# A lasting tile for the gates' weights, and decode states updated by GpSimd in whole quarters, in a hybrid mLSTM, retention and HGRN2 step

## The chip, the cores and the metric

The kernel runs on one core of one Trainium2 chip. Its engines are named as in the profile: PE multiplies matrices (PEld is its loading of weights), DVE is VectorE, ACT ScalarE, POOL GpSimd, and SP holds the queue that issues all loads and stores. The metric is the device time of one execution in microseconds (us), lower is better. Lines are those of the kernel before, unless it is said that they are of the new one, whose lines are some eight higher behind the middle of the file.

## The reference

One step of a trunk of two layers, for a prompt of 1024 tokens and for 8 sequences that decode one token each, with the same weights. Each layer projects its input once, runs three groups of heads side by side, gates them, projects the result and adds it with a LayerNorm. Shortened to what bears on the change:

```python
proj = jnp.einsum('btd,dn->btn', x, w_in)
(m_qk, m_v, m_o, m_z, m_if, r_q, r_k, r_v, r_g,
 h_f, h_i, h_q, h_g) = jnp.split(proj, _split_points(), axis=-1)
...
gates = (m_if + b_mgate).astype(f32)          # 4 heads, i and f
ig = gates[..., :M_HEADS]
lf_m = jax.nn.log_sigmoid(gates[..., M_HEADS:])
...
# mLSTM, one step (for a decoded token L = 1)
dec = jnp.exp(b[..., -1] + m - m_new)
w_s = jnp.exp(b[..., -1:] - b + igT - m_new[..., None])
C_new = dec[..., None, None] * C + jnp.einsum('bhs,bshk,bshv->bhkv', w_s, k, v)
...
# HGRN2, one step
S_new = (jnp.exp(Bc[:, -1])[..., None] * S
         + jnp.einsum('bshk,bshv->bhkv', k * jnp.exp(Bc[:, -1:] - Bc), v))
...
mix = jnp.concatenate([y_m, y_r, y_h], axis=-1).astype(x.dtype)
out = jnp.einsum('btm,md->btd', mix, w_out)
x_new = layer_norm(ALPHA * x + out, ln_g, ln_b)
```

For a decoded token the output of a head is its new state, read with the query: a sum over the key index for every value index.

## The kernel before

The prompt is worked off in two blocks, b = 0 (512 tokens and the 8 decoded ones, 520 columns in two runs of 260) and b = 1 (512 tokens). A list of sixteen steps sets their order: the three groups H (HGRN2), R (retention) and M (mLSTM) of a layer and block, and the output projections, each put between groups of the next block. In the M step of block 0 all mLSTM prompt work and its decode are issued; the chunks of 128 tokens of that step (four, `L632` scores, `L644`, `L643` and `L647` products, `L613`, `L619` transposes) then run on PE among the projections of the H step of block 1.

A tile framework gives every tile a buffer of its tag (`NBUF` says how many) and sets the waits; a scheduler that models time sets the order of each engine's instructions, and each engine then follows its own list. All loads and stores are issued in order on SP.

`project` multiplies the block's input, which is held as two rounded parts, with one 128-column tile of weights, held as two parts too: three matmul terms for each of 8 slices (`L150`). Its weights come as two halves through `load_w`: load to "st", copy on ACT (`L133`), difference on DVE (`L134`), into one of three "w" buffers, asked for ahead of the rest (`AHEAD_W`). `silu_to` takes a result out of its PSUM bank (ACT `L216`, DVE `L217`). The "gate path" below is the stretch of the M step's last projections before the chunks, with `L217` and `L588` on DVE.

`gates` is called once for each layer and block, four times. It takes one "w" buffer, clears it on POOL (`L240`), copies the 8 gate columns into it on ACT (`L242`) and their rounding error on DVE (`L243`), and multiplies (`L251`).

The decode states are worked off in quarters (a head, or a pair of half heads, by four of the eight sequences). For mLSTM, `sample_M` has 8 quarters a layer of 96 partitions x 384: it loads the state `St` and the rows of q and k, broadcast over the partitions from the DRAM tile `drow` that `token_rows` wrote (PE transposes `L694`, ACT copy, stores); POOL multiplies k by v (`L829`), DVE does `St*w + kv` for each of four sequences (`L831`), the state is stored, and DVE multiplies by q and sums in one instruction for each of four sequences (`sample_read`, `L714`, with a small read of the sum behind each). A quarter takes three of the four "smp" buffers. `sample_H` has 4 quarters a layer of 128 x 256: two products on POOL (`L744`, `L745`), the sum on DVE (`L746`), the same reading. `sample_R` is of the same shape and is not changed.

The sums of all quarters of a group are transposed, normed and gated by its `fin`, which is put into `late` and run in the H step of block 1, after its projections: PE transposes `L753`, `L778`, `L839`. Norms take the power -1/2 on POOL (`L162`). In a chunk of mLSTM POOL also does the two `L638`, and ACT `L607` and DVE `L627` read the "mb" tiles that are loaded from the DRAM tile `db`.

In HGRN2's recurrence for the prompt, DVE and PE take turns (`L391`, `L392` and `L376`), with `L463` and `L464` on POOL behind `L457` and `L458`; its tiles are of the tags "hc" and "hg". "c15" is a tag of 128 x 388 tiles for norms and token rows, "gt" one for gates' columns.

## Time and profile before

| | us |
|---|---|
| median of 3 runs | 1347.32 |
| lowest and highest | 1344.84, 1353.62 |
| the profiled execution | 1354.15 |
| its span, first to last instruction | 1352.4 |
| PE busy in it | 1286.7 |
| DVE busy | 876.2 |
| ACT busy | 593.7 |
| POOL busy | 256.2 |

The profile shows one execution, which took some 7 us more than the median. In it the mean clock granted to PE was 0.983 of the full one. In the timelines of the trace each row begins with the start and the duration in us, neighbours of one kind are put together with their count, and what stands in brackets is how long the engine was idle before and what ended it.

### The profile page before, as it was taken

The page shows a single profiled execution, that of the slowest core. Times are in us where ns is not written, and L with a number is a line of the kernel's source. Part 1 is how long each engine was busy: PE and PEld are TensorE (multiplying, and loading weights), DVE is VectorE, ACT ScalarE, POOL GpSimd, SP SyncE. Part 2 cuts the span into 40 slices and gives each one's busy share as a digit, 9 for nine tenths or more (in the row PEclk, how much of TensorE's full clock was granted, in tenths as well). Part 3 has the DMA queues.
Part 4 walks back from the last instruction along what each step waited for, and adds up shares of the span by engine and source line. Part 5 has one row for each costly group of instructions (what it writes and reads, how often), then busy time and mean ns, then how long its engine had stood idle before and what let it go on. Part 6 is the DMA issues. An engine that isn't in the chain of part 4 may idle for free. (4 is left out here: it accounts for less than half of the span.)

```text
span 1352.4 us, 30892 instructions
## 1 busy us (share of the span) xinstructions
PE 1286.7 (95%) x11888; PEld 1168.9 (86%) x11888; DVE 876.2 (65%) x2548; ACT 593.7 (44%) x1301; POOL 256.2 (19%) x261
## 2 busy tenths in 40 slices
PE   7979999988999999999999999999799999999986
PEld 7979999877898888889987999989688987888886
DVE  6566468568665656747745765875776549475775
ACT  6522455428432234736723234653564232454441
POOL 0012023012200330102210232210221014111223
PEclk9998999999999999999999999999998999999998
DMA  4543245543333452422254344555343335333252
GB/s 156 154 133 94 79 132 146 181 134 103 111 104 103 130 152 79 136 95 72 84 179 154 99 115 145 145 177 156 112 134 96 97 124 157 97 102 95 87 176 94
DMA packets 113835, 166.21 MB, mean 123 GB/s; under 512 B 21092, under 2 KB 49924, under 8 KB 113688
## 3 DMA queue, kind: packets, MB, share of 16 engines
q1 hardware_dynamic: 113688, 164.25, 39.7%
q8 instruction: 93, 1.52, 0.5%
q14 instruction: 54, 0.44, 0.1%
HBM read 140.90 MB, written 15.32 MB: 116 GB/s over the span
## 5 line engine op out<-in xcount | busy, mean ns | idle before, releaser
L150 PE MATMUL pp<-x,w 128*128 128x260 f32 (+2 forms) x6096 | 1022.9, 324 | 25.0 <-DVE w L134 5.6
L150 PEld LDWEIGHTS pp<-x,w 128*128 128x128 f32 x6096 | 874.5, 191 | 111.4 <-DVE w L134 9.1
L134 DVE TENSOR_TENSOR w<-st,w 128x512 fp32r<-128x512 f32 x344 | 251.7, 733 | 172.2 <-ACT w L133 166.9
L133 ACT CAST w<-st 128x512 fp32r<-128x512 f32 x344 | 212.6, 621 | 329.5 <-PE pp L150 279.1
L162 POOL TENSOR_TENSOR small<-small,phalf 128x4 f32<-128x4 f32 (+1 forms) x54 | 62.4, 1158 | 376.7 <-DVE small L193 193.6
L181 ACT ACTIVATE c<-pa,small,small 128x96 f32<-128x96 f32 (+1 forms) x144 | 49.9, 427 | 18.6 <-DVE small L178 18.6
L551 DVE SCALAR_TENSOR_TENSOR tmp<-tmp,prm,tmp 128x512 f32<-128x512 f32 x72 | 53.4, 742 | 3.1 <-ACT tmp L543 2.6
L831 DVE SCALAR_TENSOR_TENSOR smp<-smp,swb,smp 96x96 f32<-96x96 f32 x64 | 21.1, 378 | 39.3 <-POOL smp L829 39.3
L376 PEld LDWEIGHTS pa<-hc,hc 64*32 64x32 f32 (+1 forms) x2432 | 32.1, 109 | 16.6 <-issue 9.3
L376 PE MATMUL pa<-hc,hc 64*32 64x32 f32 (+1 forms) x2432 | 38.2, 199 | 7.3 <-DVE hc L392 5.2
L210 DVE SCALAR_TENSOR_TENSOR y<-pf,prm,y 128x128 f32<-128x128 f32 (+1 forms) x132 | 36.5, 327 | 12.8 <-PE pf L204 12.4
L216 ACT ACTIVATE tmp<-pp 128x260 f32<-128x260 f32 (+1 forms) x48 | 21.8, 455 | 42.0 <-PE pp L150 40.3
L880 DVE SCALAR_TENSOR_TENSOR y<-tmp,pp 128x260 f32<-128x260 f32 (+2 forms) x56 | 25.5, 456 | 19.9 <-PE pp L150 18.6
L463 POOL TENSOR_TENSOR x<-x 128x520 f32<-128x520 f32 (+1 forms) x12 | 16.1, 1344 | 115.3 <-DVE x L457 101.2
L829 POOL TENSOR_TENSOR smp<-smp,svs 96x384 f32<-96x384 f32 x16 | 13.2, 823 | 130.9 <-DMA smp<-drow 123.8
L941 ACT ACTIVATE t<-pa,small 128x512 f32<-128x512 f32 (+1 forms) x27 | 19.9, 774 | 40.8 <-DVE small L931 40.8
L217 DVE SCALAR_TENSOR_TENSOR y<-tmp,pp 128x260 f32<-128x260 f32 (+1 forms) x48 | 24.1, 503 | 20.2 <-ACT tmp L216 20.2
L379 DVE COPY_PREDICATED dscores<-lmask,pa 128x128 f32<-128x128 uint8 x96 | 26.9, 296 | 15.1 <-PE pa L376 14.7
L157 POOL TENSOR_TENSOR x<-y,x 128x512 fp32r<-128x512 f32 (+1 forms) x20 | 24.1, 1219 | 65.4 <-ACT x L156 65.4
L714 DVE SCALAR_TENSOR_TENSOR smp<-smp,smp 96x96 f32<-96x96 f32 (+1 forms) x160 | 33.7, 253 | 0.2
L457 DVE TENSOR_TENSOR x<-pp,tmp 128x260 f32<-128x260 f32 (+1 forms) x36 | 17.9, 510 | 24.0 <-DMA x<-x 15.8
L204 PE MATMUL pf<-ident,c 128*128 128x128 f32 (+1 forms) x132 | 29.6, 272 | 3.0 <-DVE c L196 3.0
(245 smaller groups left out, 1649.4 us busy)
## 6 DMA issues: line engine op xcount, KB each, us to landing
st<-in_w_in_dram SPq DMA_DIRECT2D x280, 256.0 KB
st<-in_w_out_dram SPq DMA_DIRECT2D x72, 256.0 KB
smp<-drow SPq DMA_DIRECT2D x64, 144.0 KB
tmp<-xres SPq DMA_DIRECT2D x16, 260.0 KB
mb<-db SPq DMA_DIRECT2D x16, 256.0 KB
tmp<-in_xT_dram SPq DMA_DIRECT2D x16, 256.0 KB
xres<-rc SPq DMA_DIRECT2D x16, 256.0 KB
out_y_prompt_dram<-t SPq DMA_DIRECT2D x16, 256.0 KB
```

The source lines that it names most:

```text
L133: A.copy(out=w[:, 0], in_=st)
L134: V.tensor_sub(out=w[:, 1], in0=st, in1=w[:, 0].bitcast(F32))
L150: PE.matmul(p, lhsT=w[k // 4][:, wp, k % 4, :], rhs=xt[:, xp, k, c0:c1], start=(k == order[0] and i == 0), stop=(k == order[-1] and i == 2))
L162: G.tensor_tensor(out=r[:n, 0:4], in0=val, in1=phalf[:n], op=ALU.pow)
L181: A.activation(out=y[:n, 96 * h:96 * h + 96], in_=ht[:, h, :], func=AF.Identity, scale=rs[:n, h:h + 1], bias=ve[:n, 4 + h:5 + h])
L204: PE.transpose(py[:, 128 * j:128 * j + n], y[:n, 128 * j:128 * j + 128], ident[:n, :n])
L210: V.scalar_tensor_tensor(out=dst, in0=py[:, 128 * j:128 * j + n], scalar=prm[:, l, pc + j:pc + j + 1], in1=dst, op0=ALU.mult, op1=ALU.mult)
L376: PE.matmul(pz[z:z + w, i, :], lhsT=k_[r, j, o + z:o + z + w], rhs=q_[r, j, o + z + d:o + z + d + w], start=True, stop=True)
L379: V.copy_predicated(Dg, lmask[:, (LEVELS + (0,)).index(h), :].unsqueeze(1).to_broadcast([128, 4, 32]), pz)
L551: V.scalar_tensor_tensor(out=acc[:, 0:512], in0=raw[:, q:q + 512], scalar=cw(q), in1=acc[:, 0:512], op0=ALU.mult, op1=ALU.add)
L714: V.scalar_tensor_tensor(out=qb[:, i, :], in0=qb[:, i, :], scalar=1.0, in1=St[:, i, :], op0=ALU.mult, op1=ALU.mult, accum_out=hs[:, i:i + 1])
L880: V.scalar_tensor_tensor(out=r2[k][:, c0:c1], in0=xr[:, c0 - r0:c1 - r0], scalar=ALPHA, in1=p, op0=ALU.mult, op1=ALU.add)
```

## The change

There are three parts. The gates' weights get a tile of their own, 128 x 8 x 100, which is cleared once at the program's start; the columns of the 8 gates are filled for block 0 of each layer and stay for block 1. In `sample_H` and `sample_M` the state is updated on POOL with operations on whole quarters, and read with one product on POOL and one sum on DVE (`sample_read_pool`, new line 718 and 719); the decay of mLSTM is a product with a broadcast column (`rows_by`, new line 723). And four tags get another number of buffers: mb 2 to 3, c15 6 to 4, hc 4 to 3, gt 2 to 1.

```diff
-NBUF = dict(pp=3, pa=4, pf=1, t2=7, tmp=4, rc=3, mb=2, c15=6, smp=4, small=10, mv=4, bst=4, hc=4, hg=2, vv=1, st=3, w=3,
-            eb=2, gt=2, mpb=2, stg=1)
+NBUF = dict(pp=3, pa=4, pf=1, t2=7, tmp=4, rc=3, mb=3, c15=4, smp=4, small=10, mv=4, bst=4, hc=3, hg=2, vv=1, st=3, w=3,
+            eb=2, gt=1, mpb=2, stg=1)
...
     def gates(l, b, xt):
         n = width(b)
-        with tc.high_priority(offset=AHEAD_W):
-            stg = mk([128, KT, 8], "stg", NBUF["stg"])
-            dma(out=stg, in_=I["w_gate"][l])
-            w = mk([128, KT, 128], "w", NBUF["w"], dt=F32R)
-            G.memset(w.bitcast(F32), 0.0)
-            for i in range(2):
-                A.copy(out=w[:, :, 32 * i:32 * i + 4], in_=stg[:, :, 4 * i:4 * i + 4])
-                V.tensor_sub(out=w[:, :, 64 + 32 * i:68 + 32 * i], in0=stg[:, :, 4 * i:4 * i + 4],
-                             in1=w[:, :, 32 * i:32 * i + 4].bitcast(F32))
+        w = wgate
+        if b == 0:
+            with tc.high_priority(offset=AHEAD_W):
+                stg = mk([128, KT, 8], "stg", NBUF["stg"])
+                dma(out=stg, in_=I["w_gate"][l])
+                for i in range(2):
+                    A.copy(out=w[:, :, 32 * i:32 * i + 4], in_=stg[:, :, 4 * i:4 * i + 4])
+                    V.tensor_sub(out=w[:, :, 64 + 32 * i:68 + 32 * i], in0=stg[:, :, 4 * i:4 * i + 4],
+                                 in1=w[:, :, 32 * i:32 * i + 4].bitcast(F32))
...
+    def sample_read_pool(hs, r, St, qb, n):
+        G.tensor_mul(out=qb, in0=qb, in1=St)
+        V.tensor_reduce(out=hs, in_=qb, axis=AX.X, op=ALU.add)
+
+    def rows_by(t, v, r, n):
+
+        G.tensor_tensor(out=t, in0=t, in1=v.unsqueeze(2).to_broadcast([r, 4, n]), op=ALU.mult)
...
                 G.tensor_mul(out=St, in0=St, in1=eb)
-                V.tensor_add(out=St, in0=St, in1=kb)
+                G.tensor_add(out=St, in0=St, in1=kb)
                 dma(out=O["hgrn_s"][l, j, hf], in_=St)
-                sample_read(hs[:, j, bs], 128, St, qb, DK)
+                sample_read_pool(hs[:, j, bs], 128, St, qb, DK)
...
-                for i in range(4):
-                    V.scalar_tensor_tensor(out=St[:, i, :], in0=St[:, i, :], scalar=wb[0:96, h, 0, 4 * hf + i:4 * hf + i + 1],
-                                           in1=kb[:, i, :], op0=ALU.mult, op1=ALU.add)
+                rows_by(St, wb[0:96, h, 0, bs], 96, DH)
+                G.tensor_add(out=St, in0=St, in1=kb)
                 dma(out=O["mC_s"][l, h, hf], in_=St)
-                sample_read(hs[0:96, h, bs], 96, St, qb, DH)
+                sample_read_pool(hs[0:96, h, bs], 96, St, qb, DH)
...
+    wgate = cp.tile([128, KT, 100], F32R, name="wgate")
+    G.memset(wgate.bitcast(F32), 0.0)
```

Since a scheduler sets the orders, the change also moves what it doesn't name. On POOL in layer 0 the decode quarters stood among the gate path and the first two chunks, with the gates' memset behind the sixth. Before, from the fifth quarter (new buffers have new numbers; `x` is the output projection's input, `rc` belongs to a chunk):

```order
L829 TENSOR_TENSOR smp_4333<-smp_4333,svs_3932 96x384
L157 TENSOR_TENSOR x_776_5574<-y_16_194,x_776_5574 128x512
L157 TENSOR_TENSOR x_776_5574<-y_195_1598,x_776_5574 128x512
L829 TENSOR_TENSOR smp_4349<-smp_4349,svs_3932 96x384
L240 MEMSET w_4475 128x1024
L162 TENSOR_TENSOR small_4001<-small_3999,phalf 128x4
L638 TENSOR_TENSOR rc_4018<-t_368_2785,rc_4018 96x256
L638 TENSOR_TENSOR rc_4018<-t_369_2786,rc_4018 96x256
L829 TENSOR_TENSOR smp_4365<-smp_4365,svs_3932 96x384
L829 TENSOR_TENSOR smp_4381<-smp_4381,svs_3932 96x384
L162 TENSOR_TENSOR small_4084<-small_4082,phalf 128x4
```

In the new kernel the same place begins behind the input of the output projection, and reads (L837 is the old L829, L839 the sum into the state):

```order
L157 TENSOR_TENSOR x_773_5526<-y_194_1590,x_773_5526 128x512
L837 TENSOR_TENSOR smp_4261<-smp_4261,svs_3924 96x384
L723 TENSOR_TENSOR smp_4271<-smp_4271,swb_3886 96x384
L839 TENSOR_TENSOR smp_4259<-smp_4259,smp_4261 96x384
L718 TENSOR_TENSOR smp_4260<-smp_4260,smp_4259 96x384
L162 TENSOR_TENSOR small_3993<-small_3991,phalf 128x4
L638 TENSOR_TENSOR rc_4010<-t_367_2777,rc_4010 96x256
L638 TENSOR_TENSOR rc_4010<-t_368_2778,rc_4010 96x256
L837 TENSOR_TENSOR smp_4273<-smp_4273,svs_3924 96x384
L723 TENSOR_TENSOR smp_4283<-smp_4283,swb_3886 96x384
L839 TENSOR_TENSOR smp_4271<-smp_4271,smp_4273 96x384
L718 TENSOR_TENSOR smp_4272<-smp_4272,smp_4271 96x384
```

The memset is gone; a whole quarter, with the next one's product L723 drawn into it, stands before each chunk's power L162, and the eight quarters lie over the four chunks.

On DVE, the gate path of layer 0 (L217 and L588 empty the projections' banks, L134 makes weights) had the third and fourth quarter's updates and reads in it:

```order
L831 SCALAR_TENSOR_TENSOR smp_4299<-smp_4299,swb_3894,smp_4301 96x96 x4
L714 SCALAR_TENSOR_TENSOR smp_4300,shs_580_4266<-smp_4300,smp_4299 96x96 x4
L217 SCALAR_TENSOR_TENSOR y_375_2792<-tmp_3784,pp_3759 128x260
L134 TENSOR_TENSOR w_3822<-st_3820,w_3822 128x512
L217 SCALAR_TENSOR_TENSOR y_375_2792<-tmp_3812,pp_3787 128x260
L831 SCALAR_TENSOR_TENSOR smp_4315<-smp_4315,swb_3894,smp_4317 96x96 x3
L134 TENSOR_TENSOR w_4403<-st_4401,w_4403 128x512
L831 SCALAR_TENSOR_TENSOR smp_4315<-smp_4315,swb_3894,smp_4317 96x96
L714 SCALAR_TENSOR_TENSOR smp_4316,shs_580_4266<-smp_4316,smp_4315 96x96 x4
L588 SCALAR_TENSOR_TENSOR y_375_2792<-tmp_3850,y_375_2792 128x260
L134 TENSOR_TENSOR w_4408<-st_4406,w_4408 128x512
L588 SCALAR_TENSOR_TENSOR y_375_2792<-tmp_3878,y_375_2792 128x260
```

The same projections in the new order:

```order
L217 SCALAR_TENSOR_TENSOR y_374_2784<-tmp_3776,pp_3751 128x260
L134 TENSOR_TENSOR w_3814<-st_3812,w_3814 128x512
L217 SCALAR_TENSOR_TENSOR y_374_2784<-tmp_3804,pp_3779 128x260
L134 TENSOR_TENSOR w_4363<-st_4361,w_4363 128x512
L588 SCALAR_TENSOR_TENSOR y_374_2784<-tmp_3842,y_374_2784 128x260
L134 TENSOR_TENSOR w_4368<-st_4366,w_4368 128x512
L588 SCALAR_TENSOR_TENSOR y_374_2784<-tmp_3870,y_374_2784 128x260
L134 TENSOR_TENSOR w_4399<-st_4397,w_4399 128x512
L622 TENSOR_TENSOR c_520_3949<-pa_3945,gt_386 128x288
L624 TENSOR_SCALAR c_520_3949<-pa_3945,gt_386 128x96
L634 TENSOR_TENSOR mb_3931<-pa_3957,mb_3931 128x512
```

No decode instruction is left between them. The eight sums L719 stand later, one or two a chunk; the first of them is the third row here, among the statistics (L171) of the first chunk:

```order
L171 BN_AGGR mv_3982<-bst_3981 128x2 x3
L719 TENSOR_REDUCE shs_579_4258<-smp_4260 96x4
L627 SCALAR_TENSOR_TENSOR mb_4174<-mb_4174,gt_386,negm 128x128
L176 SCALAR_TENSOR_TENSOR small_3991<-small_3977,mv_3982 128x4
L627 SCALAR_TENSOR_TENSOR mb_4174<-mb_4174,gt_386,negm 128x128 x2
L609 COPY small_4015<-rc_4010 96x4
L627 SCALAR_TENSOR_TENSOR mb_4174<-mb_4174,gt_386,negm 128x128
L134 TENSOR_TENSOR w_4504<-st_4502,w_4504 128x512
L178 SCALAR_TENSOR_TENSOR small_3991<-mv_3982,small_3993 128x4
```

So behind the chunk's statistics a wait for POOL's first quarter now stands ahead of the mask L627 and of L176, the input of the norm's power.

On PE in layer 0, the transposes of the decode's q rows (pa_3901) and k rows (pa_3912) stood together, ahead of the gate path's last projections:

```order
L150 MATMUL pp_3523<-x_1_66,w_3492 128x260 x12
L694 MATMUL pa_3901<-ident,t_368_2785 8x96 x2
L694 MATMUL pa_3901<-ident,t_369_2786 8x96 x2
L694 MATMUL pa_3912<-ident,t_370_2787 8x96
L150 MATMUL pp_3561<-x_1_66,w_3553 128x260 x2
L694 MATMUL pa_3912<-ident,t_370_2787 8x96
L694 MATMUL pa_3912<-ident,t_371_2788 8x96 x2
L613 MATMUL pa_3948<-ident,vv_2789 128x128 x2
L150 MATMUL pp_3561<-x_1_66,w_3553 128x260 x10
```

Now those of the k rows (pa_3904) stand behind all of them, right before the first chunk's L632:

```order
L150 MATMUL pp_3845<-x_1_66,w_3814 128x260 x12
L694 MATMUL pa_3904<-ident,t_369_2779 8x96 x2
L694 MATMUL pa_3904<-ident,t_370_2780 8x96 x2
L613 MATMUL pa_3940<-ident,vv_2781 128x128 x3
L619 MATMUL pa_3945<-ident,t_369_2779 128x128 x2
L619 MATMUL pa_3945<-ident,t_370_2780 128x128
L632 MATMUL pa_3957<-t_367_2777,t_369_2779 128x128 x2
L632 MATMUL pa_3957<-t_368_2778,t_370_2780 128x128 x2
```

What moved is the start of the k rows: in the trace of before they stood 35 us ahead of the first L632 (252.6 against 287.88 us). At the second chunk the gates of block 1 stood so before:

```order
L150 MATMUL pp_4447<-x_428_3266,w_4444 128x512 x7
L632 MATMUL pa_4042<-t_368_2785,t_370_2787 128x128 x2
L632 MATMUL pa_4042<-t_369_2786,t_371_2788 128x128 x2
L150 MATMUL pp_4447<-x_428_3266,w_4444 128x512 x5
L251 MATMUL pp_4486<-x_428_3266,w_4475 100x512 x10
L643 MATMUL pa_4050<-Cst_167,rc_4018 128x97
L251 MATMUL pp_4486<-x_428_3266,w_4475 100x512 x2
```

and now so:

```order
L150 MATMUL pp_4407<-x_427_3258,w_4404 128x512 x12
L251 MATMUL pp_4438<-x_427_3258,wgate 100x512 x3
L632 MATMUL pa_4034<-t_367_2777,t_369_2779 128x128 x2
L632 MATMUL pa_4034<-t_368_2778,t_370_2780 128x128 x2
L251 MATMUL pp_4438<-x_427_3258,wgate 100x512 x8
L643 MATMUL pa_4042<-Cst_169,rc_4010 128x97
```

The gates read the lasting tile, and a part of them runs ahead of the chunk's scores. Ahead of the final transposes (L753 before, L761 in the new kernel) PE now has 14 more of the projections' 512-column matmuls. On SP the loads of the decode quarters and those of weights, about two a quarter, now take turns over the four chunks, and in the gate path only weights are loaded.

## Rows read from the trace of the kernel before

**Rows 1.** The page's busy time, share and instructions of each engine.

```profile
PE 1286.7 (95%) x11888; PEld 1168.9 (86%) x11888; DVE 876.2 (65%) x2548; ACT 593.7 (44%) x1301; POOL 256.2 (19%) x261
```

**Rows 2.** The list of PE's waits: for whom, us in total, times, longest.

```profile
PE pp L251 <- DVE small L178: 7.4, 2, 3.9
```

**Rows 3.** Timeline of PE, layer 0: start, us, what, idle before and its releaser.

```profile
252.20 0.41 PE L694 MATMUL pa<-ident,t 96*8 96x96 f32 x3
...
266.70 11.94 PE L150 MATMUL pp<-x,w 128*128 128x260 f32 x94 [0.41 <-DVE y L217]
281.95 6.10 PE L150 MATMUL pp<-x,w 128*128 128x260 f32 x36 [3.31 <-DVE y L217]
287.88 1.06 PE L632 MATMUL pa<-t,t 96*128 96x128 f32 x8
...
307.48 3.93 PE L251 MATMUL pp<-x,w 128*100 128x512 f32 x10 [3.50 <-DVE small L178]
...
340.20 4.66 PE L150 MATMUL pp<-x,w 128*128 128x512 f32 x19
...
358.60 0.38 PE L753 MATMUL pa<-ident,shs 128*8 128x128 f32 x2
```

**Rows 4.** Timeline of PE at the same place of layer 1.

```profile
936.47 4.55 PE L150 MATMUL pp<-x,w 128*128 128x260 f32 x36 [0.70 <-DVE y L217]
...
962.24 4.10 PE L251 MATMUL pp<-x,w 128*100 128x512 f32 x10 [3.89 <-DVE small L178]
```

**Rows 5.** Two stretches: us, busy PE, PEld, DVE, ACT, POOL, granted clock, DMA.

```profile
283.30:286.60 3.30, 3.30 (x17) 3.30 (x17) 0.54 (x3) 0.47 (x2) 0.82 (x1) 0.50 0.53 164
...
962.50:965.80 3.30, 3.30 (x9) 2.28 (x8) 1.46 (x4) 3.27 (x7) 2.22 (x3) 0.50 0.60 187
```

**Rows 6.** Timeline of POOL in layer 0.

```profile
263.29 0.82 POOL L829 TENSOR_TENSOR smp<-smp,svs 96x384 f32<-96x384 f32 x1 [26.14 <-DMA smp<-drow]
...
303.05 0.82 POOL L829 TENSOR_TENSOR smp<-smp,svs 96x384 f32<-96x384 f32 x1 [7.13 <-DMA smp<-in_s_C_dram]
303.81 0.95 POOL L240 MEMSET w<- 128x1024 f32 x1
...
317.69 0.82 POOL L829 TENSOR_TENSOR smp<-smp,svs 96x384 f32<-96x384 f32 x1 [7.04 <-DMA smp<-drow]
```

**Rows 7.** Timeline of ACT around the second block's gates, layer 0.

```profile
304.95 1.28 ACT L607 ACTIVATE rc<-mb,mpb 96x128 f32<-96x128 f32 x4 [3.35 <-DMA mb<-db]
306.14 0.32 ACT L242 CAST w<-stg 128x32 fp32r<-128x32 f32 x2
```

**Rows 8.** Timeline of DVE in the gate path of layer 0.

```profile
265.07 0.53 DVE L815 TENSOR_REDUCE sden<-c 8x4 f32<-8x384 f32 x1
...
279.84 1.00 DVE L831 SCALAR_TENSOR_TENSOR smp<-smp,swb,smp 96x96 f32<-96x96 f32 x4 [5.28 <-POOL smp L829]
...
281.48 0.42 DVE L217 SCALAR_TENSOR_TENSOR y<-tmp,pp 128x260 f32<-128x260 f32 x1
```

**Rows 9.** DVE's instructions by line and form: count, busy us, mean ns, idle.

```profile
L714 DVE SCALAR_TENSOR_TENSOR smp<-smp,smp 96x96 f32<-96x96 f32 x128 | 26.4, 246 | 0.1
...
L831 DVE SCALAR_TENSOR_TENSOR smp<-smp,swb,smp 96x96 f32<-96x96 f32 x64 | 21.1, 378 | 39.3 <-POOL smp L829 39.3
```

**Rows 10.** Timeline of all engines, HGRN2 recurrence of layer 0.

```profile
125.54 0.69 DVE L134 TENSOR_TENSOR w<-st,w 128x512 fp32r<-128x512 f32 x1 [1.89 <-ACT w L133]
...
127.57 1.31 POOL L463 TENSOR_TENSOR x<-x 128x520 f32<-128x520 f32 x1 [6.29 <-DVE x L457]
127.69 1.74 DVE L134 TENSOR_TENSOR w<-st,w 128x512 fp32r<-128x512 f32 x1
```

**Rows 11.** Timeline of all engines at an HGRN2 decode quarter.

```profile
85.86 1.13 DVE L714 SCALAR_TENSOR_TENSOR smp<-smp,smp 128x64 f32<-128x64 f32 x1
...
90.36 0.60 PE L376 MATMUL pa<-hc,hc 64*32 64x32 f32 x32 [2.76 <-DVE hc L392]
```

**Rows 12.** Timeline of PE at the program's start.

```profile
34.05 9.66 PE L150 MATMUL pp<-x,w 128*128 128x260 f32 x74 [1.53 <-ACT w L133]
```

## The prediction

> **What bounds the kernel now.** The page's busy line comes first: PE is busy 1286.7 us of 1352.4, 95% [rows 1], so the time moves only with what PE waits for and with the speed of its matmuls. The list of PE's waits, read next, has at its top the gates' matmuls L251: twice, 7.4 us [rows 2]. The timeline of PE gives both places, a wait of 3.50 us in layer 0 and 3.89 in layer 1, and a third of the same kind ahead of the last piece of the gate path: 3.31 us behind DVE's L217 in layer 0, 0.70 in layer 1 [rows 3, 4]. The view by stretches adds a second price: right after such an idle time PE ran 3.3 us at a granted clock of 0.50, which is the lower of its two levels, 1.2 GHz [rows 5]. Work done at half speed for 3.3 us loses 1.65 us.
>
> What ends those waits is read on the other engines. On POOL the first quarter of the mLSTM decode (L829) starts at 263.29 after 26.14 us of waiting for its rows from DRAM, the sixth starts at 303.05 after 7.13 us for its state, and the gates' memset L240 stands right behind it, from 303.81 to 304.76 [rows 6]. Then ACT: L607 waits for a load of mb until 304.95, and only behind it comes L242, the copy of the gate weights, at 306.14 [rows 7]; its result is subtracted by DVE at L243 and PE starts at 307.48. So the gates wait for a memset behind a decode quarter, and behind a load of mb on ACT. In the gate path DVE stands 5.28 us at L831 for POOL, runs the four L831 and four L714, and only then reaches L217, at 281.48, which frees PE's bank at 281.95 [rows 3, 8].
>
> **A. The lasting gate tile.** For block 1 no memset, copy or subtraction is left, so L251 can't wait for them. That takes away 3.50 + 3.89 = 7.39 us and the slow stretch behind each; one is shown for layer 1 [rows 5] and I take the same in layer 0: 2 x 1.65. **-10.7**. What is late next there is L607, whose load came at 304.95, and through it L638 and L643. Here the third mb buffer bears on it: in the new order DVE's L627 of the fourth chunk stands where that of the second stood, so the load is far ahead. Were it not, a part of the 3.50 us would come back at L643 (bounds 0 and +2 a layer, the upper an estimate, half the wait). Layer 1's block-0 gates still load, into a tile that the block before is done with. At the start the gates no longer take one of three w buffers; PE's first wait for a weight is 1.53 us [rows 12]. Bounds 0 and -1.5, and I take **-0.7**, since L133 there may as well wait for its load. The new memset runs once, ahead of all matmuls on the idle POOL: nothing.
>
> **B. The gate path without decode.** In DVE's new order no decode instruction is left between L217, L588 and L134 of the gate path. This removes 3.31 us and 1.65 of half speed behind it [rows 3, 5], 0.41 at the L217 before (266.70 in the same view, [rows 3]), and 0.70 in layer 1 [rows 4]: **-6.1**. Late next is L134 itself, whose weights come a buffer ahead; it takes 0.69 us against some 3 us of PE for each half weight, so I leave nothing for it.
>
> **C. The HGRN2 decode.** Four quarters a layer lose their four L714 on DVE. One of these took 1.13 us, and the recurrence behind it on DVE held PE for 2.76 us [rows 11]. All of it goes to POOL, where an L829 takes 0.82 us [rows 6] and these tiles are smaller. **-2.8**, bounds 0 and -4.4 (with its half speed); I leave out the latter since L463 and L464, which feed the same recurrence, now stand behind three more operations a quarter on POOL.
>
> **D. The mLSTM decode comes later.** This is the largest unknown. Before, the k rows' transposes (L694) ended at 252.6 and the first L829 ran at 263.29: 10.7 us [rows 3, 6]. In the new PE order the k rows' L694 stand right before the first L632, some 1.1 us ahead of it, and the eight quarters lie over the four chunks, no longer half of them over the gate path. So the first quarter starts at L632 + 10.7 - 1.1 - 1 = L632 + 8.6 (the 1, an estimate with bounds 0 and 2, is for the four q rows that are written ahead). The pace before was (317.69 - 263.29)/7 = 7.77 us a quarter [rows 6]. A quarter's own work was 0.82 of L829 and 1.64 of L831 and L714 (279.84 to 281.48), 2.5 us [rows 6, 8]; now it is three or four POOL operations of 0.82 and a reduce of 0.53 (that of L815, 384 elements a row [rows 8]), 3.0 to 3.8 us, with the fourth being the next quarter's multiply. So the pace grows by 0.5 to 1.3; I take **8.5 us**, with bounds 7.0 (should the DVE queue have been what held it) and 9.1. The last reduce ends at 8.6 + 7 x 8.5 + 3.8 = 71.9 us behind the first L632.
>
> PE reaches L753, the first of the final transposes that need all decode, 358.60 - 287.88 = 70.7 us after L632 [rows 3]; less the 3.50 + 1.65 of A that is 65.6. The new order puts 14 more L150 ahead, of 4.66/19 = 0.245 us each [rows 3], so PE is there at 69.0. It waits 2.9 us a layer, **+5.8** (0 to 7 a layer), with two stretches at half speed behind it, **+3.3**. The decode's DVE work falls: 64 L831 and 128 L714, 21.1 + 26.4 us [rows 9], become 16 reduces of 0.53. POOL takes 48 x 0.82 us more, beside its 256.2 [rows 1]; DVE is off PE's path there, so this is worth nothing by itself.
>
> On the shared use of SBUF the trace has this: DVE's L134 took 0.69 us alone and 1.74 beside POOL's L463 [rows 10]. It is in the pace's upper bound and in rival 3. The Trainium skill, SBUF — State Buffer, "Who interferes with whom", says that a DVE operation with two inputs in SBUF and GpSimd's reads exclude one another, while a reduce on this chip never does; the trace agrees in the first with the 1.74 us, and no run here yet shows the second. By that rule the new reduces would run free, and each of the 48 new GpSimd operations could hold an L134: at an L829's 0.82 us that is 39 us of DVE by the end, on PE's path only where weights come late.
>
> **E. Buffers.** c15 from 6 to 4 and hc from 4 to 3 make some norms and the recurrence wait for a free tile: in the new DVE order the second half's L392 stands behind the first's last step. No row prices this; PE's waits at L376 and L204 are the nearest and are below 3 us apiece. **+1**, bounds 0 and 3.
>
> Sum: -10.7 - 0.7 - 6.1 - 2.8 + 5.8 + 3.3 + 1 = -10.2. The profiled execution took 1354.15 us, so it would be 1344.0; it lies 6.8 above the median of the runs, and from that, 1347.32, I get **1337**. About 1%, 13.5 us, is what a measurement of this kernel can tell from no change.
>
> **Rivals.** (1) *The decode keeps ahead.* At the old pace, 7.77, the last reduce ends at 8.6 + 54.4 + 3.8 = 66.8, before PE's 69.0; it decides at a pace of 8.1. Then D and E fall away and -20.3 is left: **1327**. For it: half of the pace before may have been DVE's queue, with L831 standing behind L134 and L157. Against: a quarter's k rows take their buffer from the quarter before, so load and four operations follow one another.
>
> (2) *The waits only move.* On POOL the norms' power L162 and both L638 of each chunk now stand behind a quarter's L718, which waits for DRAM. At the upper pace, 9.1, the third quarter's L718 comes 8.6 + 18.2 + 3.3 = 30 us after L632, when the second chunk's power is wanted; the last reduce is then 7.1 us late, and some 3 us more a layer go to L162, L638 (2 x 1 us) and L643 behind it: 20 us in all, as much as A to C give. **1347**. For it: before, too, POOL's waits on DRAM were what held others [rows 6, 8]. Against: a chunk comes every 17 us, and two quarters at 8.5 just fit.
>
> (3) *Slower, by shared SBUF.* If each of a quarter's four POOL operations is stretched by 0.5 us, half of what L463 cost an L134 (1.74 - 0.69, [rows 10]), the pace is 10.5. The last reduce then ends at 8.6 + 73.5 + 3.8 = 85.9, 16.9 late: 33.8 in both layers, +3.3 and +1 against -20.3 gives +18: **1365**. It decides, against a kernel that is no slower, at 8.1 + 8/7 = 9.2 us a quarter. For it: L134 runs all through that stretch. Against: a quarter in four meets an L134 only for part of its time. The rule named above would make this the likelier, the more L134 stands beside the quarters; the pair of [rows 10] shows that it can happen, not how often.
>
> **How the numbers follow.** The forecast has 0.45, rival 1 0.27, rival 2 0.17, rival 3 0.11. The predicted time is the forecast's, 1337. Its own bounds, with D at 0 to 14 and A, C and E at some of their ends: 1329 to 1347. The range reaches down past rival 1, less its C bound, to 1324, and up past rival 2 to 1355; below and above are left a tenth each. Faster by over 1% means under 1333.8: nearly all of rival 1 and a fifth of the forecast, 0.36; slower means above 1360.8: rival 3, of which some lies lower, 0.09 with a little of rival 2; within 1% is the rest, 0.55.
>
> **What the profile after would show.** A: no wait at L251 in block 1, no half clock behind it. B: no wait over 1 us for L217 in the gate path. D: the first multiply of the quarters some 8 to 9 us after the first L632, a pace near 8.5, and one wait of some 3 us at the final transposes of each layer, ended by the decode's reduce. Rival 1: no such wait. Rival 2: waits of L204 or L643 behind L162 or L638. Rival 3: POOL operations well above 0.82 us and L134 above 0.69 in that stretch. The forecast is wrong if the pace lies outside 7 to 9.1, or if the loads on SP's queue, where the quarters' now alternate with the weights', hold L150 for weights: nothing before shows what that costs.

## The result, and the profile after

The changed kernel takes 1357.76 us (median of 22 runs), the kernel before, in as many runs beside it, 1349.49: a ratio of 1.0063 (1.0047 to 1.0078), 0.6% slower. Forecast were 10 us less. The profiled execution took 1359.73 us.

```profile
PE 1290.0 (95%) x11888; PEld 1171.4 (86%) x11888; DVE 865.8 (64%) x2304; ACT 591.4 (44%) x1297; POOL 323.6 (24%) x322
```

PE is busy 3.3 us more than before [rows 1]; POOL has 67 us more. PE's idle time, the sum of the list of its waits, grew by 2.7 us only (54.1 to 56.8), so the second thing to read is the clock. From each run's time and mean granted clock one can split it: time x (1 - clock) is what the slow level took away, the rest is the time at full clock. Averaged over the runs the changed kernel lost 28.2 us to the clock, with 1329.2 at full clock; the kernel before lost 20.8 to 22.5 in the five sessions below, with 1327 to 1331. The split is rough, since it also counts slow stretches in which PE had no work. Counting PE's busy time alone, the two profiles lost 17.4 and 22.9 us, and their spans differ by 5.6. So nearly all of the change is work at the lower clock.

Where: PE's waits in the changed kernel have no L251 (7.4 us in [rows 2]) and almost no L217. New ones stand for POOL's L638, for the norm (L181) and for the decode's last sum L719:

```profile
PE pa L643 <- POOL rc L638: 5.8, 2, 4.5
...
PE pf L204 <- ACT c L181: 3.6, 4, 2.4
...
PE pa L846 <- DVE shs L719: 2.9, 1, 2.9
...
PE pp L150 <- DVE y L217: 0.8, 1, 0.8
```

The timeline of PE in layer 0, answering to [rows 3]:

```profile
276.19 0.49 PE L694 MATMUL pa<-ident,t 96*8 96x96 f32 x4
...
277.18 1.06 PE L632 MATMUL pa<-t,t 96*128 96x128 f32 x8
...
291.41 0.86 PE L251 MATMUL pp<-x,wgate 128*100 128x512 f32 x3
...
330.21 0.64 PE L643 MATMUL pa<-Cst,rc 96*128 96x97 f32 x2 [4.47 <-POOL rc L638]
...
347.58 0.48 PE L204 MATMUL pf<-ident,c 128*128 128x128 f32 x1 [2.41 <-ACT c L181]
...
354.79 0.38 PE L761 MATMUL pa<-ident,shs 128*8 128x128 f32 x2
...
359.54 1.46 PE L150 MATMUL pp<-x,w 128*128 128x260 f32 x10 [1.44 <-DVE w L134]
362.38 0.46 PE L376 MATMUL pa<-t,t 64*32 64x32 f32 x32 [1.39 <-DVE dscores L379]
363.37 0.45 PE L376 MATMUL pa<-hc,t 64*32 64x32 f32 x32 [0.53 <-DVE dscores L379]
364.70 0.38 PE L204 MATMUL pf<-ident,c 8*128 8x8 f32 x2 [0.88 <-DVE c L196]
```

The k rows' L694 are right before L632, and the gates run without a wait. Then PE waits 4.47 us at the fourth chunk's L643, 2.41 at a norm, and behind the final transposes 1.44, 1.39, 0.53 and 0.88. What held L643 is on POOL, answering to [rows 6], with DVE beside it (first POOL, then DVE):

```profile
285.10 0.98 POOL L837 TENSOR_TENSOR smp<-smp,svs 96x384 f32<-96x384 f32 x1 [4.16 <-DMA smp<-drow]
...
322.13 0.82 POOL L837 TENSOR_TENSOR smp<-smp,svs 96x384 f32<-96x384 f32 x1 [3.58 <-DMA smp<-drow]
322.91 3.56 POOL L723 TENSOR_TENSOR smp<-smp,swb 96x384 f32<-96x384 f32 x1
326.43 0.98 POOL L839 TENSOR_TENSOR smp<-smp,smp 96x384 f32<-96x384 f32 x1
327.50 0.99 POOL L718 TENSOR_TENSOR smp<-smp,smp 96x384 f32<-96x384 f32 x1
328.45 1.01 POOL L162 TENSOR_TENSOR small<-small,phalf 128x4 f32<-128x4 f32 x1
329.44 1.40 POOL L638 TENSOR_TENSOR rc<-t,rc 96x256 f32<-96x256 f32 x2
...
350.53 0.82 POOL L837 TENSOR_TENSOR smp<-smp,svs 96x384 f32<-96x384 f32 x1 [3.81 <-DMA smp<-drow]
```

```profile
323.43 0.14 DVE L176 SCALAR_TENSOR_TENSOR small<-small,mv 128x4 f32<-128x4 f32 x1
323.50 0.67 DVE L134 TENSOR_TENSOR w<-st,w 128x512 fp32r<-128x512 f32 x1
...
324.17 0.67 DVE L364 TENSOR_TENSOR hc<-t,t 128x512 f32<-128x512 f32 x1
324.77 0.41 DVE L392 TENSOR_TENSOR hc<-t,t 128x256 f32<-128x256 f32 x1
```

The first quarter starts 7.9 us behind L632 (forecast 8.6) and the pace is (350.53 - 285.10)/7 = 9.35 us (forecast 8.5, upper bound 9.1). The third chunk's L176, the input of the norm's power, is done at 323.6; but on POOL L162 stands behind a whole quarter, whose L723 took 3.56 us instead of 0.82 while DVE ran L134, L364 and L392 on two SBUF tiles each. L162 starts at 328.45, the first of the two L638 follows at 329.44, and PE goes on at 330.21. Had L723 taken 0.82 us, all this would have come 2.7 us earlier (an estimate, 3.56 less 0.82): so of the 4.47 us at L643 more than half is the stretched operation and the rest the queue.

The clock is read from stretches right after the final transposes of both layers:

```profile
364.50:378.10 13.60, 13.40 (x206) 12.26 (x207) 6.75 (x35) 4.42 (x17) 1.66 (x2) 0.50 0.09 29
1016.40:1023.20 6.80, 6.13 (x47) 5.75 (x47) 6.26 (x25) 3.32 (x8) 3.01 (x3) 0.50 0.63 191
1026.70:1040.30 13.60, 13.60 (x220) 12.10 (x206) 7.22 (x32) 4.38 (x17) 0.51 (x1) 0.50 0.07 22
```

The same places of the kernel before: full speed in layer 0, and 10.2 us in layer 1.

```profile
358.60:372.20 13.60, 12.22 (x326) 10.83 (x325) 10.39 (x55) 6.14 (x24) 5.37 (x5) 1.00 0.35 111
1023.90:1034.10 10.20, 10.20 (x136) 9.41 (x127) 5.48 (x26) 3.37 (x15) 0.00 (x0) 0.50 0.01 2
```

Half speed for 13.6 us loses 6.8 us. Behind a wait the prediction had counted 3.3 us [rows 5]; here it is four times that. It does not take several short waits: gate_alone, a run told of below, has one wait of 2.52 us at this place, for a norm, and then

```profile
357.30:380.90 23.60, 22.57 (x330) 19.70 (x331) 14.65 (x63) 9.33 (x30) 6.97 (x5) 0.50 0.27 83
```

### The profile page after: what moved, and what is told of

It is laid out like the page before. It is cut to its first block, busy times and chain, and to the rows that moved or that the text cites. A ratio compares the mean times of both kernels' runs of the same rounds, so it can differ in the third digit from the quotient of the medians.

```text
span 1358.0 us, 30694 instructions
## 1 busy us (share of the span) xinstructions
PE 1290.0 (95%) x11888; PEld 1171.4 (86%) x11888; DVE 865.8 (64%) x2304; ACT 591.4 (44%) x1297; POOL 323.6 (24%) x322
## 4 chain that ended last, share of the span: by engine, by line
PE 57%; DMA 13%; DVE 10%; issue 7%; POOL 7%; ACT 3%; SPq 3%; POOLq 0%; DVEq 0%; ACTq 0%
PE pp L150 44%; DMA smp<-drow 5%; PE pa L376 2%; DVE w L134 2%; DMA st<-in_w_out_dram 2%; DMA st<-in_w_in_dram 1%; POOL smp L839 1%; DMA x<-x 1%; ACT w L133 1%; POOL small L162 1%; DMA out_hgrn_s_dram<-smp 1%; POOL smp L778 1%; DVE tmp L551 1%; POOL smp L837 1%; PE pa L414 1%
## 5 line engine op out<-in xcount | busy, mean ns | idle before, releaser
L134 DVE TENSOR_TENSOR w<-st,w 128x512 fp32r<-128x512 f32 x344 | 254.2, 742 | 180.6 <-ACT w L133 177.3
L133 ACT CAST w<-st 128x512 fp32r<-128x512 f32 x344 | 212.4, 621 | 316.7 <-PE pp L150 249.7
L162 POOL TENSOR_TENSOR small<-small,phalf 128x4 f32<-128x4 f32 (+1 forms) x54 | 59.5, 1104 | 352.4 <-DVE small L193 190.7
L181 ACT ACTIVATE c<-pa,small,small 128x96 f32<-128x96 f32 (+1 forms) x144 | 50.1, 431 | 33.6 <-DVE small L178 33.5
L719 DVE TENSOR_REDUCE shs<-smp 96x4 f32<-96x384 f32 (+1 forms) x24 | 12.1, 505 | 50.2 <-POOL smp L718 46.0
L887 DVE SCALAR_TENSOR_TENSOR y<-tmp,pp 128x260 f32<-128x260 f32 (+2 forms) x56 | 25.6, 458 | 26.5 <-PE pp L150 26.1
L217 DVE SCALAR_TENSOR_TENSOR y<-tmp,pp 128x260 f32<-128x260 f32 (+1 forms) x48 | 24.2, 508 | 27.5 <-ACT tmp L216 27.5
L216 ACT ACTIVATE tmp<-pp 128x260 f32<-128x260 f32 (+1 forms) x48 | 21.9, 456 | 39.4 <-PE pp L150 37.4
L382 ACT COPY scores<-dscores 32x128 f32<-32x128 f32 x64 | 19.0, 296 | 28.2 <-DVE dscores L379 27.5
```

What stands on the lines that cost most here:

```text
L133: A.copy(out=w[:, 0], in_=st)
L134: V.tensor_sub(out=w[:, 1], in0=st, in1=w[:, 0].bitcast(F32))
L162: G.tensor_tensor(out=r[:n, 0:4], in0=val, in1=phalf[:n], op=ALU.pow)
L181: A.activation(out=y[:n, 96 * h:96 * h + 96], in_=ht[:, h, :], func=AF.Identity, scale=rs[:n, h:h + 1], bias=ve[:n, 4 + h:5 + h])
```

## The experiments

The theory after reading the result, Q: on POOL a chunk's power and L638 stand behind whole quarters, since the decode starts late. Its rivals: S, POOL and DVE stretch each other on SBUF; L, or M with the third mb buffer as its cause, the late start itself costs, in whatever form the quarters are worked off; C, the loss is the low clock behind the final transposes; P, SP's queue, held at a store until a quarter's sum is done, brings loads late.

Ratios are to the kernel before in the same session, with 95% intervals; "lost" is the mean of time x (1 - clock) over the runs. In the same sessions the kernel before lost 20.8 to 22.5 us.

| kernel | gate tile | mb | mLSTM on | HGRN2 on | ratio | lost us |
|---|---|---|---|---|---|---|
| after | yes | 3 | POOL | POOL | 1.0063 (1.0047 to 1.0078) | 28.2 |
| buffers_alone | no | 3 | DVE | DVE | 1.0047 (1.0028 to 1.0066) | 29.9 |
| mb3_only | no | 3 | DVE | DVE | 1.0057 (1.0033 to 1.0080) | 28.4 |
| gate_alone | yes | 3 | DVE | DVE | 1.0005 (0.9987 to 1.0023) | 25.4 |
| after_no_H | yes | 3 | POOL | DVE | 1.0086 (1.0062 to 1.0110) | 26.5 |
| after_no_M | yes | 3 | DVE | POOL | 1.0003 (0.9986 to 1.0021) | 23.8 |
| decode_alone | no | 2 | POOL | POOL | 1.0092 (1.0066 to 1.0117) | 30.6 |
| after_mb2 | yes | 2 | POOL | POOL | 1.0020 (1.0001 to 1.0040) | 23.6 |
| gate_mb2 | yes | 2 | DVE | DVE | 0.9982 (0.9966 to 0.9998) | 19.1 |
| best_try | yes | 2 | DVE | POOL | 1.0007 (0.9983 to 1.0030) | 26.5 |
| mb3_early | no | 3, early | DVE | DVE | 0.9994 (0.9974 to 1.0015) | 25.5 |
| gate_early | yes | 3, early | DVE | DVE | 0.9970 (0.9947 to 0.9993) | 26.4 |
| noM_early | yes | 3, early | DVE | POOL | 1.0009 (0.9988 to 1.0029) | 25.4 |
| after_early | yes | 3, early | POOL | POOL | 1.0095 (1.0070 to 1.0120) | 27.9 |
| after_MV | yes | 3 | DVE, whole quarters | POOL | 1.0052 (1.0032 to 1.0072) | 28.5 |
| after_638v | yes | 3 | POOL | POOL | 1.0037 (1.0019 to 1.0056) | 26.8 |
| after_smp5 | yes | 3 | POOL | POOL | 1.0114 (1.0086 to 1.0143) | 32.6 |
| after_store_pool | yes | 3 | POOL | POOL | 1.0115 (1.0090 to 1.0141) | 28.0 |
| after_fill | yes | 3 | POOL | POOL | 1.0072 (1.0047 to 1.0098) | 23.8 |

**The parts by themselves.** The edits put single hunks of the change back or in.

buffers_alone: `NBUF` of the change in the kernel before.

> Only the four buffer numbers (mb 3, c15 4, hc 3, gt 1); gates and decode as before. The k rows' transposes stand late in the order here too. Theory Q: the late start with short quarters on POOL costs little, and the gates' memset still waits: within 4 us of before, 1346 to 1353. Rival L (the late start costs the time): 1354 or more. Theory S: no change from before, since no work is moved between POOL and DVE.

It is 0.5% slower, outside what Q gave: a part priced at +1 us costs 6.

gate_alone: the change with both decodes as before.

> The lasting gate tile and the new buffer numbers, with both decode states worked off as before (one product on POOL for mLSTM, the rest on DVE). The k rows' transposes stand late, as in the changed kernel. Theory Q: POOL's quarters are short (0.82 us), so the chunks' power waits little, and the gates' wait is gone: 1338 to 1343, 7 to 11 us under before. Theory S: the gain of the gates is the same, so also 1338 to 1343; a rival L (the late start alone costs the time, whoever works off the quarters): 1352 or more.

Missed: level with before. Against buffers_alone the tile gives back 0.42%, 5.7 us, half of what was forecast. It can't be by the wait at L251: in the profile of buffers_alone the list of PE's waits has none there, though its gates are the old ones. What the tile does here instead is open.

decode_alone: the two decode hunks, with old gates and buffers.

> Only the decode on POOL in whole quarters; gates and buffers as before, so the decode starts early, in the gate path, and the gates' memset stands in POOL's queue behind quarters that are now longer. Theory Q: the gates' wait stays or grows by 1 to 3 us a layer, the chunks' power waits less than in the changed kernel: 1350 to 1356. Theory S: 5 to 9 us over before, with POOL operations well above 0.82 us over the whole decode: 1355 to 1359.

12 us slower, more than either gave; 9 of them are clock. So an early start does not save this form either.

after_no_H and after_no_M: the HGRN2, or the mLSTM, hunk put back in the changed kernel.

> The changed kernel with the HGRN2 decode as before; the mLSTM decode on POOL. Theory Q (the mLSTM quarters in POOL's queue are what costs): as slow as the changed kernel, within 2 us, 1356 to 1360 if before is at 1352. A rival H (the HGRN2 decode on POOL, ahead of L463 and L464, costs a part): 3 us or more below the changed kernel.

> The changed kernel with the mLSTM decode as before; the HGRN2 decode on POOL. Theory Q: as fast as the kernel with gates and buffers alone, 1352 to 1354, or up to 3 us below it by the prediction's part C. Rival H: 1356 or more.

Without the HGRN2 part the change is slower still (by 0.23%, 3 us; the intervals overlap), without the mLSTM part it is level with before. So the mLSTM part costs 0.60%, 8 us, beside the HGRN2 part on POOL; without it, from gate_alone to after_no_H, it costs 0.81%, 11 us. Rival H falls.

**The third mb buffer.** after_mb2 is the change with

```diff
-... mb=3, c15=4 ...
+... mb=2, c15=4 ...
```

> The whole change, but with 2 mb buffers as before instead of 3. In the order the transposes of the decode's k rows then stand 240 projection matmuls ahead of the first chunk again, so that the quarters begin in the gate path. Theory Q (the queue: POOL's whole quarters lie over the chunks because the decode starts late, each chunk's power and L638 stand behind a quarter, and PE waits for them): no wait of PE for L638, time some 8 to 12 us under the changed kernel, 1346 to 1350 against 1349 of before. Theory S (shared SBUF stretches POOL and DVE whenever a quarter runs): the same POOL work meets DVE elsewhere, the time stays within 3 us of the changed kernel, 1355 to 1361.

5.8 us less than the change, nearer to Q than to S; but the wait for L638, which Q saw gone, is 7.6 us in its profile. mb3_only is the kernel before with `mb=3, c15=5`:

> The kernel before with 3 mb buffers instead of 2, and c15 5 instead of 6 to make room; nothing else. The buffers' kernel was 5 to 6 us slower than before though its time at full clock was 1.6 us lower: its mean granted clock was 0.978 against 0.984. Theory M (the third mb buffer makes the scheduler start the decode late, and the late start brings the slow clock): 1356 to 1360 against 1352 of before, mean clock 0.978 to 0.980. Theory B (the smaller hc, gt and c15 do it): 1350 to 1353, clock 0.983 or more.

As M expected. In its profile the last quarter, in the old form, is late too: DVE's L831 waits for it beyond the moment at which PE wants the final transposes, L649 stands behind it on DVE and is what PE's L839 waits for, and behind the transposes PE waits again (PE, then DVE):

```profile
352.44 0.80 PE L839 MATMUL pa<-ident,shs 96*8 96x96 f32 x4 [2.75 <-DVE Cst L649]
...
360.73 0.39 PE L150 MATMUL pp<-x,w 128*128 128x260 f32 x1 [2.07 <-ACT x L156]
```

```profile
349.40 1.00 DVE L831 SCALAR_TENSOR_TENSOR smp<-smp,swb,smp 96x96 f32<-96x96 f32 x4 [3.47 <-POOL smp L829]
```

mb3_early keeps that buffer and issues the rows early:

```diff
-        d, (qr, kr) = sample_qk(QH, KH)
+        with tc.high_priority(offset=AHEAD_W):
+            d, (qr, kr) = sample_qk(QH, KH)
```

> The kernel before with 3 mb buffers and c15 5, and the decode's rows issued at a high priority (k rows again 127 matmuls ahead of the chunks). Theory M: the 5.7 per mille of the third buffer are gone: 0.997 to 1.002 of before. Rival: 1.004 to 1.007, as with the third buffer alone.

0.999: the cost is gone with the buffer in place. So it is the order that costs, which the scheduler chose once it had a third buffer, and not the buffer. But the clock did not come back, as M would have it: this kernel still loses 25.5 us to it, beside 20.8 of before in its session, and behind its final transposes, at which PE did not wait, it runs a slow stretch too:

```profile
363.00:376.60 13.60, 13.60 (x209) 12.48 (x209) 6.33 (x32) 4.42 (x17) 1.12 (x2) 0.51 0.06 21
```

What is less is the time at full clock, 1322.7 us beside 1327.6. So that the late start itself costs is argued: the early rows may as well bring a gain of their own, which covers a loss that stays. They were not run without the third buffer.

**The mLSTM decode in whole quarters.** after_early is the change with the same three lines.

> The whole change, with the transposes and the writing of the mLSTM decode's q and k rows issued at a high priority. In the order the k rows' transposes then stand 127 projection matmuls (16 us) ahead of the first L632 instead of right before it, and three of the eight quarters lie ahead of the first chunk's power on POOL. Theory M (the late start costs the time): 3 to 7 us under the changed kernel, 1.001 to 1.004 of before, the slow stretch behind the final transposes of layer 0 gone. Rival (the third buffer itself, its loads or the smaller hc): as the changed kernel, 1.005 to 1.008.

M falls for this form: an early start does not make it faster. PE stands 5.48 us at a norm (PE, then all engines):

```profile
306.42 0.47 PE L204 MATMUL pf<-ident,c 128*128 128x128 f32 x1 [5.48 <-ACT c L181]
```

```profile
296.87 0.55 DVE L719 TENSOR_REDUCE shs<-smp 96x4 f32<-96x384 f32 x1 [1.99 <-POOL smp L718]
...
299.45 0.16 DVE L176 SCALAR_TENSOR_TENSOR small<-small,mv 128x4 f32<-128x4 f32 x1
...
299.69 1.01 POOL L162 TENSOR_TENSOR small<-small,phalf 128x4 f32<-128x4 f32 x1 [2.85 <-DVE small L609]
302.10 1.28 ACT L607 ACTIVATE rc<-mb,mpb 96x128 f32<-96x128 f32 x4 [4.00 <-DMA mb<-db]
...
302.53 2.34 DVE L627 SCALAR_TENSOR_TENSOR mb<-mb,gt,negm 128x128 f32<-128x128 f32 x3 [2.85 <-ACT rc L607]
...
304.80 0.78 DVE L178 SCALAR_TENSOR_TENSOR small<-mv,small 128x4 f32<-128x4 f32 x1
```

DVE's L719 waits for the third quarter, and behind it stand L170 to L176 and POOL's L162. But L162 is done at 300.7, and the norm goes on only at 304.80: its L178 stands on DVE behind L627, which waits for L607, and L607 waits 4.00 us for a load of mb that SP issued at 297.13, behind that quarter's store at 295.78. So here it is a load, and not POOL's queue, that ends the wait last.

after_638v puts one line on DVE:

```diff
-                    G.tensor_tensor(out=qw[0:96, 2 * hp:2 * hp + 2, :], ...
+                    V.tensor_tensor(out=qw[0:96, 2 * hp:2 * hp + 2, :], ...
```

> The changed kernel with the two L638 of each mLSTM chunk on DVE instead of POOL (the power L162 stays on POOL). Theory Q (a chunk's POOL work stands behind a quarter, and PE's L643 waits for it: 4.47 and 1.35 us in the trace): the wait of L643 for POOL is gone, that of L204 for the norm stays; 3 to 6 us under the changed kernel. Theory S (the quarters stretch by shared SBUF) and the rest of the clock's loss at the final transposes: within 2 us of the changed kernel.

3.5 us less, as Q expected, though the intervals overlap; PE's wait for L638 fell to 1.4 us, but its waits for weights at L134 rose to 14.8 (5.9 in the change).

after_MV gives decay, sum and product of the mLSTM quarters to DVE: `rows_by`, `tensor_add` and `tensor_mul` on V.

> The changed kernel with the mLSTM quarters' decay, sum and product with q on DVE, in the same whole-quarter operations; POOL keeps the product of k and v, and the HGRN2 decode. The start is late as in the changed kernel. Theory Q and S (POOL's queue, or POOL and DVE together on SBUF, costs the 8 us): the time falls to that of the kernel without the mLSTM part, 1.000 to 1.002 of before. Rival (the late whole quarters cost, on whichever engine): 1.005 or more.

The rival holds: 1.5 us less than the change, within the interval. All engines, in its layer 0:

```profile
338.47 0.82 POOL L837 TENSOR_TENSOR smp<-smp,svs 96x384 f32<-96x384 f32 x1 [6.00 <-DMA smp<-drow]
339.32 0.55 DVE L839 TENSOR_TENSOR smp<-smp,smp 96x384 f32<-96x384 f32 x1 [1.58 <-POOL smp L837]
...
340.15 0.56 DVE L723 TENSOR_TENSOR smp<-smp,swb 96x384 f32<-96x384 f32 x1 [0.28 <-DMA smp<-in_s_C_dram]
...
340.63 0.15 DVE L176 SCALAR_TENSOR_TENSOR small<-small,mv 128x4 f32<-128x4 f32 x1
...
340.86 1.39 POOL L162 TENSOR_TENSOR small<-small,phalf 128x4 f32<-128x4 f32 x1 [1.57 <-DVE small L176]
...
342.22 1.40 POOL L638 TENSOR_TENSOR rc<-t,rc 96x256 f32<-96x256 f32 x2
...
342.99 0.74 PE L643 MATMUL pa<-Cst,rc 96*128 96x97 f32 x2 [5.28 <-POOL rc L638]
```

POOL's L837 waits 6.00 us for its rows, DVE then waits for L837 and for the state's load, with the chunk's L176 behind it, and L643 comes 5.28 us late. It is a quarter that waits for its loads in the queue ahead of the chunk's chain, on either engine; DVE's pieces are short here, 0.56 us at most, so their length is not what holds the chain.

after_smp5 has `smp=5`:

> The changed kernel with 5 smp buffers instead of 4, so that a quarter's loads can start earlier. In the trace a quarter came every 9.3 us, of which POOL waited 3.4 to 4.4 us for its rows. Theory Q: the pace falls to 8 us or less, the last quarter ends well ahead of the final transposes, and the time falls by 3 to 7 us. Theory S: POOL's operations, not the loads, set the pace, and it stays within 0.5 us of 9.3, the time within 2 us.

```profile
290.10 0.82 POOL L837 TENSOR_TENSOR smp<-smp,svs 96x384 f32<-96x384 f32 x1 [2.32 <-DVE c L822]
...
340.52 0.82 POOL L837 TENSOR_TENSOR smp<-smp,svs 96x384 f32<-96x384 f32 x1 [1.40 <-DMA smp<-drow]
```

```profile
PE pp L150 <- ACT w L133: 11.6, 8, 4.7
```

Pace (340.52 - 290.10)/7 = 7.2 us, as Q expected, and yet 7 us slower than the change: PE now waits for weights, 11.6 us at L133 (5.3 in the change). A quicker decode alone is no gain; both theories missed the time.

after_store_pool issues a store elsewhere:

```diff
-                dma(out=O["mC_s"][l, h, hf], in_=St)
+                G.dma_start(out=O["mC_s"][l, h, hf], in_=St)
```

> The changed kernel with the stores of the mLSTM quarters' states issued by POOL behind its own sum, instead of by SP. Theory P (SP's queue, held at a store until the quarter's sum is done, brings loads late): SP's 44 us of waiting at the stores are gone, and the time falls by 3 us or more, to 1.004 of before or less. Theory Q (the chunk's power and L638 behind the quarter on POOL): no gain, or a loss of up to 5 us by POOL's time for issuing 16 stores: 1.006 to 1.010.

In the change SP's queue stood at these stores (SP's waits, of the change and of this kernel):

```profile
SPq L840 <- POOL smp L839: 44.3, 16, 6.0
```

```profile
SPq L836 <- POOL smp L839: 38.3, 14, 5.8
SPq L836 <- DMA out_mC_s_dram<-smp: 28.3, 11, 3.3
```

7 us slower than the change. But SP's wait is not gone, as P needs: it waits for the same sum, and for the store's end, at the next load into the buffer, 66.6 us in all instead of 44.3, and POOL is busy 0.58 us with issuing each store. So the run doesn't tell P from Q, and P stays open.

**The clock.** after_fill adds, in the first steps of the recurrence of block 1 (h < 4, first half):

```diff
+                    fill = pa()
+                    for k in range(3):
+                        PE.matmul(fill[0:100, :], lhsT=wgate[:, k, 0:100], rhs=X[1][:, 0, k, 0:512], ...
```

> The changed kernel with 18 added 512-column matmuls a layer (2 x 18 x 0.245 = 8.8 us of PE), whose result nobody reads, between the first steps of the HGRN2 recurrence of block 1, where PE had three waits of 0.9 to 1.4 us and then ran 13.7 us at half clock in layer 0, and 20.5 us in layer 1. Theory C (the loss is the slow clock behind these waits): the half-clock stretch behind the final transposes goes or shrinks by 10 us or more a layer, the mean clock rises from 0.979 to 0.984 or more, and the time falls by 0 to 6 us though work is added. Rival (the waits themselves): the clock stays and the time rises by 4 to 9 us.

Between the two: 4.4 us less are lost to the clock, 9.7 more are spent at full clock (8.4 more than the kernel before in the same session), about the 8.8 us of the added work. In the profile the slow stretch of layer 1 shrank from 20.5 to 6.8 us, that of layer 0 did not. Work in the gaps held the clock up in one layer of two, and cost more than it saved. That the clock is the loss in the other kernels is read from their clocks, not shown by this run.

**Put together.** gate_mb2 is the kernel before with the tile, and `c15=4` to make room.

> The kernel before with the lasting gate tile, and c15 4 instead of 6 to make room; 2 mb buffers, decode as before, with its early start. By the terms of the prediction the gates' wait (7.4) and the two half-speed stretches behind it (3.3) are gone: 1340 to 1344 against 1352 of before. Rival W (the next thing there, the load of mb that L607 waits for, ends the wait instead): the waits move to L643 or L644 and 3 to 6 us are left, 1346 to 1349.

W, roughly: 0.998, 2.4 us, a little less than W left. The gates' wait is gone, and others come in its place (5.3 and 5.6 us for weights before):

```profile
PE pp L150 <- ACT w L133: 9.2, 8, 2.9
PE pp L150 <- DVE w L134: 7.2, 10, 2.3
...
PE pa L643 <- POOL rc L638: 3.5, 2, 1.9
```

best_try, noM_early and gate_early are gate_mb2 with the HGRN2 decode on POOL; after_no_M with early rows; and gate_alone with early rows.

> Put together from what helped: the lasting gate tile, the HGRN2 decode on POOL, the mLSTM decode as before, 2 mb buffers, c15 4, hc 4, gt 2. The gate tile with 2 mb buffers was at 0.998 of before, and the HGRN2 part was worth 3 us beside the mLSTM part and nothing alone. Expected: 0.995 to 0.998 of before; if the HGRN2 decode on POOL delays L463 in this order, 0.998 to 1.001.

> The changed kernel with the mLSTM decode as before and its rows issued at a high priority: gate tile, new buffers, HGRN2 decode on POOL, no late start. Theory M: 0.995 to 0.998 of before, the late start's cost gone from a kernel that stood at 1.000. Rival: 0.999 to 1.002.

> The lasting gate tile and the new buffers with both decodes as before, and the mLSTM decode's rows issued at a high priority. Against the kernel with the third buffer and the same priority (0.999 of before) it tells what the gate tile is worth without the late start. By the prediction's part A (gates' wait gone): 0.992 to 0.995. Rival (the third mb buffer has already ended that wait, the tile adds little): 0.997 to 1.001.

The first two missed and lie where their second expectation had them: without the mLSTM part the HGRN2 part is worth nothing, or costs. gate_early is the best of all, 0.997 (0.9947 to 0.9993) of before, 1346.85 us beside 1350.11 in its session, and faster than the change. That is the edge of the rival's range: with the third buffer L251 doesn't wait in mb3_early, without the tile, and the tile adds little.

## Why the prediction was wrong

**B and E, as they were sized.** The prediction took the gate path without decode as a pure gain (-6.1) and the buffers as +1. They are one thing: the third mb buffer makes the scheduler put the decode late, and buffers_alone, which holds both, is 6.4 us slower, not 5 faster. The gain is there (no wait for L217 in its list), but the late decode of the old form already ends behind the final transposes, as the profile of mb3_only shows, and the loss is in the clock: 29.9 us beside 21.9 of before. D charged a late end to POOL's form alone. This is the step that failed, by 11.5 us; that the loss comes by the late end, and by no other change of the order, is argued: mb3_early got the time back with the clock still low.

**A, size and cause.** The wait at L251 went, as forecast, but not by the tile alone: of the kernels with the old gates, buffers_alone, mb3_only, mb3_early and decode_alone have no such wait either, since their order is another. So A counted a wait that the new order ends anyway. The tile is worth 5.7 us beside the new buffers, 2.4 with the old ones and 3.2 with the early start (mb3_early to gate_early, in two sessions, with other c15, hc and gt), not 11.4. In gate_mb2, where it does take the wait away, other waits came up in its place. Only with both decodes on POOL does it come near, 9.7 us from decode_alone to after_mb2, which differ in c15, hc and gt too.

**C.** -3 us in the whole change, as forecast, with intervals that overlap; between nothing and +5 without the mLSTM part (gate_early to noM_early). The 1.13 us it was read from was one slow L714 of 32, whose mean was 0.28.

**D, right in sum by luck.** +8 us for the mLSTM part, where 5.8 + 3.3 were counted. The start (7.9 for 8.6) was right; the pace, 9.35 us, lies above the bound of 9.1, which the prediction named as a sign that it is wrong. One reason is that it gave all four POOL operations 0.82 us, while L839 and L718 take 1.0 even where nothing stretches them. And in layer 0 PE did not wait at the last sum: it had been held before, at L643 and the norms, by POOL's queue, which is rival 2's mechanism; the 2.87 us at L719 came in layer 1 only. The stretch of L723 is rival 3's, on single operations; by the prediction's rule from the Trainium skill, SBUF — State Buffer, "Who interferes with whom", a reduce would stay free, and the L719 at 328.52, beside POOL's L162, took 0.55 us (0.53 counted).

**Half speed.** Counted at 1.65 us behind a wait. Of the 8 us of loss some 6 are clock, in stretches of up to 13.6 us.

In the rivals' sums, rival 1 lets E fall away with D and gives no reason; with E it is 1328 instead of 1327.

Left open: why the HGRN2 part helps in one order and costs in another, and what of it is the order's chance; the differences there are 3 to 5 us, with intervals of 3. Open too is what makes the slow stretches behind the final transposes so long.

## What to carry to other kernels

With a scheduler, test each buffer count by itself: one more mb buffer, with one c15 less, put a decode's start 32 us later beside the chunks (24.6 us ahead of the first L632, then 7.0 behind it) and cost nearly as much as the rewritten code. Where an engine follows its queue in order, side work that waits for loads holds all that stands behind it: a quarter ahead of a norm's power held PE on POOL and on DVE alike. And price a wait by the slow stretch behind it at that place of the program, not by its own length.

## What the runs showed of the hardware

PE's waits of 1.44, 1.39, 0.53 and 0.88 us within 7 us were followed by 13.6 us at a granted clock of 0.50, the 1.2 GHz level, although PE was then busy 13.4 of 13.6 us. The number of waits doesn't decide how long it lasts: behind single waits of 3.31 and 3.89 us of the kernel before 3.3 us are shown [rows 3 to 5], behind one of 2.52 us in gate_alone 23.6, with PE busy for 22.57 of them. And one L723, 0.82 us where nothing stretched it, took 3.56 while DVE ran operations on two SBUF tiles.
